# Residual of row blocks 6 and 3 held apart in DRAM and added in SBUF, with plain stores; gates of row block 3 on GpSimd; another order of the last steps

## The chip, the core and the metric

The kernel runs on one NeuronCore of a Trainium2 chip. The core has five instruction streams that run side by side and meet at semaphores: TensorE (PE, with its weight loads shown as PEld), VectorE (DVE), ScalarE (ACT), GpSimd (POOL) and SyncE (SP), which only issues transfers here. Each stream executes its instructions strictly in the order in which the program lists them. Sixteen DMA engines move data between DRAM and the on-chip memory SBUF; matmul results land in PSUM banks of 128x512 float32.

The metric is the device time of one launch in microseconds (us). Before the change it is 1100.19 us, the median of three runs (1099.69 to 1100.69).

## The reference

One layer of a hybrid decoder over 1024 tokens of width 1024, all in float32. Only the last sub-layer matters here:

```python
    h = rmsnorm(x, pre_w_mlp[l]) * (1.0 + sc2) + sh2
    u = jnp.square(jax.nn.relu(h @ w_up[l]))
    x = x + g2 * rmsnorm(u @ w_down[l], post_w_mlp[l])
```

Here `x` on the right is the residual that the first sub-layer produced, and `rmsnorm(y, w)` is `y / sqrt(mean(y^2) + eps) * w`, with the mean over the 1024 columns of a row.

## The kernel before

The 1024 rows (tokens) are cut into eight row blocks, 0 to 7, of 128 rows each; a row block has two halves of 512 columns. The product with `w_down` is computed with a seven-product scheme (Strassen's), which pairs row block t with row block t+4, for t = 0 to 3. `ORDER` names the seven products 1, 5, 6, 3, 7, 2, 4. `PLAN` (L1480) says for each product which PSUM bank it accumulates in ("a", "b" or "c"), whether it starts that bank, and to which accumulator its content is added afterwards. A bank holds a running sum: in bank "a" product 1 is followed by 6, then by 7, then by 4, and after each of these the bank is read out and added to a different accumulator. So product 6 of a pair may not start on PE before DVE has read the bank as product 1 left it. The accumulators are `accs[tb][half]`, 128x512 tiles in SBUF, one for each row block and half.

The contraction runs in five groups of 128-row blocks. The change touches the last group (g = 4, two blocks; each product is six matmuls of 512 columns) and what follows it. The list `order` (L1586) interleaves the products of the pairs t = 0, 1, 2 over steps 0 to 20, and steps 21 to 23 are products 1, 5, 6 of the pair t = 3. `last_rows` (L1621) holds the remaining four products of t = 3 (row blocks 3 and 7) by hand.

At each step the code lists the product's matmuls, then the read-out of the product of the step before (`accum`, DVE: accumulator += bank), then whatever was put down for this step with `on(step, fn)`. When the last addition to a half of a row block is done, a chain of small steps follows, spread over the next steps of the list:

- `square(tb, half)`: ACT squares the half and sums each row (the sum is fetched by a second instruction, ACTIVATION_READ_ACCUMULATOR);
- `gated(tb, half)`: DVE multiplies the half by `gw2`, the product of gate and norm weight, in place, so it must come after the square has read it;
- `root(tb)`: DVE adds the two halves' sums (TENSOR_SCALAR, 128x1), POOL raises the result to the power -0.5;
- `scaled(tb, half)`: ACT multiplies the half by that factor, a scalar for each row;
- `onto_x(tb)`: POOL issues two DMAs that add the halves onto `out` in DRAM, where the residual was stored long before (L1027). POOL is busy while it issues one.

The residual of three halves, (3,1), (7,0) and (7,1), is not stored to `out` but to a DRAM tile `x1d`, and loaded back to SBUF ahead of the end (L1278); there DVE multiplies by the factor and adds the residual in one SCALAR_TENSOR_TENSOR, and SP or ACT issue a plain store.

Engines are pinned, so each runs its instructions in the order of the listing; a scheduler places SP's plain stores. All operations go through one helper (L39), which is therefore the line that the profile shows for nearly everything.

Of the kernel before, what the change touches and what calls it, by code (L numbers as in the profile page):

```python
# [47 lines left out]
def hybrid_layer(ctx: ExitStack, tc: tile.TileContext, I, out, dbg=None):  # L48
# [31 lines left out]
    def m_(name, shape=(P, 512), dt=F32):  # L80
        return M.tile(list(shape), dt, tag="m", name=name)
# [10 lines left out]
    def tp_ps(name):  # L92
        return pb.tile([P, 512], F32, tag="b", name=name)
# [905 lines left out]

    x2ctx = ExitStack()  # L1000
    X2 = x2ctx.enter_context(tc.tile_pool(name="poolX2", bufs=1))
    x1d = dram.tile([P, 3 * 512], F32, tag="x1d", name="x1d")
    hold = {(3, 1): slice(0, 512), (7, 0): slice(512, D), (7, 1): slice(D, D + 512)}
    xn2 = [None] * TB

    def out_proj(tb):
# [264 lines left out]
    for i, (g, n) in enumerate(stages):  # L1271
# [3 lines left out]
        if 10 <= i and gates:  # L1275
            entry_gate(*gates.pop(0))
        ends.append(len(seq))
    for i in range(3):  # L1278
        seq.append((f"x1_{i}", lambda i=i: x1d[:, i * 512:i * 512 + 512], None))

    def load_ahead():
# [339 lines left out]
    def last_rows():  # L1621
        a, b, t = 3, 7, 3
        ss = small.tile([P, 3], F32, tag="ssl", bufs=1, name="ssl")
        one = {n: small.tile([P, 1], F32, tag="l_" + n, bufs=1, name="l_" + n) for n in ("part", "r")}
        h = [slice(0, 512), slice(512, D)]
        ba, bc, bb, bx = bk["a", 3], bk["c", 3], tp_ps("pdlb"), tp_ps("pdlx")
        gl = [m_(f"gl{half}") for half in range(2)]
        ga0, ga = m_("ga0"), m_("ga")
# [20 lines left out]
        rest(nstep + 2)  # L1649
        acp = [accs[b][0][:, 256 * i:256 * i + 256] for i in range(2)]  # L1650
        dmm(bx[:, 0:256], g, 4, t, True, slice(0, 256))
        dmm(bx[:, 256:512], g, 4, t, True, slice(256, 512))
        for step in sorted(later):
            rest(step)
        add(accs[b][1], ba)
        sq(accs[b][1], ss[:, 0:1])
        root(a)
        add(accs[b][0], ba)
        for i in range(2):
            add(acp[i], bx[:, 256 * i:256 * i + 256])  # L1660
            sq(acp[i], ss[:, 1 + i:2 + i], 256)
        ACT.activation(ga0, ga0, AF.Copy, scale=rr_[a][:, 0:1])
        DVE.tensor_tensor(gl[1], accs[b][1], gw2[:, h[1]], ALU.mult)
# [3 lines left out]
        POOL.dma_start(out[a * P:(a + 1) * P, h[0]], ga0, accum_op=ALU.add)  # L1667
        DVE.tensor_tensor(gl[0], accs[b][0], gw2[:, h[0]], ALU.mult)
        xa, xl = take(), [take() for _ in range(2)]
        DVE.scalar_tensor_tensor(ga, ga, rr_[a][:, 0:1], xa, ALU.mult, ALU.add)  # L1670
        nc.sync.dma_start(out[a * P:(a + 1) * P, h[1]], ga)
        for half in range(2):
            DVE.scalar_tensor_tensor(gl[half], gl[half], one["r"][:, 0:1], xl[half], ALU.mult, ALU.add)
            (nc.sync if half else nc.scalar).dma_start(out[b * P:(b + 1) * P, h[half]], gl[half])

    last_rows()

# [66 lines left out]
```

## Time and profile before

| What | Value |
|---|---|
| Time, median of 3 runs | 1100.19 us |
| Span of the profiled execution, first to last instruction | 1097.6 us |
| PE busy | 1076.2 us (98%) |
| DVE busy | 795.1 us (72%) |
| ACT busy | 584.6 us (53%) |
| POOL busy | 373.2 us (34%) |

The profiled execution has its own time, of which the span is what the profile can show. 1097.6 us is 2.6 us below the median of the runs. Differences are worked out in the span and put onto the median. In a timeline row stand the start in us from the span's beginning, the duration in us (for several instructions merged, from the first start to the last end, or their sum), the engine, the line, the operation, out<-in, shapes, the count, and in brackets the idle time before it with what ended it. In a row of windows stand the stretch, its length, the busy time of PE, PEld, DVE, ACT and POOL with the number of instructions in brackets, the granted TensorE clock as a share of full speed, the busy share of the DMA engines and GB/s moved. A DMA issue row gives its queue's engine, the count, the size, and the us from issue to landing.

### The profile page before, as it was taken

The page shows a single profiled execution, that of the slowest core. Times are in us where ns is not written, and L with a number is a line of the kernel's source. Part 1 is how long each engine was busy: PE and PEld are TensorE (multiplying, and loading weights), DVE is VectorE, ACT ScalarE, POOL GpSimd, SP SyncE. Part 2 cuts the span into 40 slices and gives each one's busy share as a digit, 9 for nine tenths or more (in the row PEclk, how much of TensorE's full clock was granted, in tenths as well). Part 3 has the DMA queues.
Part 4 walks back from the last instruction along what each step waited for, and adds up shares of the span by engine and source line. Part 5 has one row for each costly group of instructions (what it writes and reads, how often), then busy time and mean ns, then how long its engine had stood idle before and what let it go on. Part 6 is the DMA issues. An engine that isn't in the chain of part 4 may idle for free.

```text
span 1097.6 us, 16208 instructions
## 1 busy us (share of the span) xinstructions
PE 1076.2 (98%) x5547; PEld 878.2 (80%) x5547; DVE 795.1 (72%) x1323; ACT 584.6 (53%) x1206; POOL 373.2 (34%) x499
## 2 busy tenths in 40 slices
PE   8999999999999999999999999999999999999995
PEld 6788776778888888888888888888888888888884
DVE  4365777878865574559776767876767787899876
ACT  3445544364565764566655555556664543555434
POOL 1153211033324663432543444533333333310014
PEclk9999999999999999999999999999999999999998
DMA  9701301534310352324577676767998888998537
GB/s 347 265 7 57 117 1 43 181 101 140 125 56 11 108 182 96 125 79 144 194 246 249 233 259 227 257 216 244 320 364 289 275 299 259 337 308 272 169 76 131
DMA packets 101587, 203.37 MB, mean 185 GB/s; under 512 B 13025, under 2 KB 13681, under 8 KB 101505
## 3 DMA queue, kind: packets, MB, share of 16 engines
q1 hardware_dynamic: 85968, 154.52, 41.4%
q0 software_dynamic: 15392, 47.57, 14.3%
q8 instruction: 43, 0.70, 0.3%
q14 instruction: 40, 0.32, 0.1%
q10 hardware_dynamic: 144, 0.26, 0.1%
HBM read 147.25 MB, written 55.05 MB: 184 GB/s over the span
## 4 chain that ended last, share of the span: by engine, by line
PE 92%; DVE 3%; ACT 1%; DMA 1%; POOL 1%; issue 1%; SPq 0%; DVEq 0%; POOLq 0%; ACTq 0%
PE pda L39 16%; PE pua L39 14%; PE pdc L39 8%; PE po L39 8%; PE puc L39 7%; PE pu L39 4%; PE pdb L39 4%; PE pq L39 4%; PE phg L39 4%; PE phq L39 3%; PE pub L39 3%; PE phf L39 3%; PE pv L39 3%; PE pk L39 2%; PE o L39 1%; PE sc L39 1%
## 5 line engine op out<-in xcount | busy, mean ns | idle before, releaser
L39 POOL TENSOR_TENSOR b<-b,b 128x512 f32<-128x512 f32 x64 | 89.6, 1400 | 222.8 <-DMA b<-w_dn 222.4
L39 ACT ACTIVATE dw<-dwr 128x512 fp32r<-128x512 f32 x72 | 45.4, 630 | 46.5 <-DMA dwr<-td 32.4
L39 ACT ACTIVATE s<-s 128x512 f32<-128x512 f32 x84 | 53.0, 631 | 31.8 <-DVE s L39 30.5
L39 DVE TENSOR_TENSOR dw<-dwr,dw 128x512 fp32r<-128x512 f32 x72 | 53.6, 744 | 9.0 <-ACT dw L39 8.9
L39 DVE TENSOR_TENSOR acc<-pda,acc 128x512 f32<-128x512 f32 x68 | 46.5, 684 | 13.7 <-PE pda L39 13.3
L39 POOL DMA_DIRECT2D td<-b x64 | 36.3, 567 | 21.6 <-POOL b L39 18.7
L39 POOL TENSOR_TENSOR rrf<-ssf,mhalf 128x1 f32<-128x1 f32 x7 | 7.9, 1253 | 95.3 <-DVE ssf L39 95.3
L39 DVE TENSOR_TENSOR wt<-s,wt 128x512 fp32r<-128x512 f32 x42 | 37.2, 886 | 2.6 <-ACT wt L39 2.5
L39 ACT ACTIVATE s<-pua 128x512 f32<-128x512 f32 x28 | 16.7, 598 | 39.4 <-PE pua L39 33.9
L39 ACT ACT_TABLE_LOAD x28 | 35.9, 1283 | 1.2 <-PEq L1737 0.7
L39 DVE SCALAR_TENSOR_TENSOR macc<-wada,cs,macc 128x512 f32<-128x512 f32 x42 | 33.7, 803 | 3.4 <-DMA wada<-wada 2.9
L39 POOL DMA_DIRECT2D b<-w_dn x64 | 34.4, 540 | 0.0
L39 POOL TENSOR_TENSOR comb<-comb,rd 128x512 f32<-128x512 f32 x8 | 11.7, 1458 | 63.3 <-DVE rd L39 44.2
L39 PE MATMUL pua<-bt_0h,wt 128*128 128x512 f32 x84 | 32.7, 389 | 0.0
L39 PE MATMUL pua<-bt_1h,wt 128*128 128x512 f32 x84 | 32.7, 389 | 0.0
L39 PE MATMUL pua<-bt_3h,wt 128*128 128x512 f32 x84 | 32.7, 389 | 0.0
L39 PE MATMUL pua<-bt_2h,wt 128*128 128x512 f32 x84 | 32.7, 389 | 0.0
L39 DVE TENSOR_TENSOR wt<-a,wt 128x512 fp32r<-128x512 f32 x42 | 31.0, 738 | 0.9 <-ACT wt L39 0.9
L39 DVE TENSOR_TENSOR acc<-pdc,acc 128x512 f32<-128x512 f32 x36 | 24.6, 684 | 8.5 <-PE pdc L39 8.4
L39 ACT ACTIVATE wt<-s 128x512 fp32r<-128x512 f32 x42 | 26.3, 626 | 8.2 <-DVE s L39 8.0
L39 PE MATMUL pda<-dw,du_6h 128*128 128x512 f32 x96 | 29.6, 389 | 0.0
L39 PE MATMUL pda<-dw,du_7h 128*128 128x512 f32 x96 | 29.5, 389 | 0.0
(757 smaller groups left out, 3746.1 us busy)
## 6 DMA issues: line engine op xcount, KB each, us to landing
dur<-ud SPq DMA_DIRECT2D x112, 256.0 KB, 4.5
wada<-wada SPq DMA_DIRECT2D x64, 256.0 KB, 3.5
b<-w_dn POOLq DMA_DIRECT2D x64, 256.0 KB, 5.2
td<-b POOLq DMA_DIRECT2D x64, 256.0 KB, 3.3
dwr<-td SPq DMA_DIRECT2D x64, 256.0 KB, 4.3
a<-w_u SPq DMA_DIRECT2D x56, 256.0 KB, 4.4
dwr<-w_dn SPq DMA_DIRECT2D x48, 256.0 KB, 4.5
ud<-s SPq DMA_DIRECT2D x42, 256.0 KB, 3.6
```

Source lines behind the costliest of these rows:

```text
L39: ins = op(*args, **kw)
```

## The change

Row block 6 (both halves) and half (3,0) join the three halves whose residual is kept in `x1d`: six halves instead of three. They are loaded back by SP, and `with_x` adds them in SBUF, followed by a plain store. So the accumulating DMAs of (6,0), (6,1) and (3,0) are gone, and with them three of ACT's scalings; one scaling, of (3,1), is new, since its residual is added by POOL. The gates of row block 3 move from DVE to POOL. In `last_rows` product 7 comes ahead of 3, product 4 accumulates onto bank "a" in place of a bank of its own (`pdlx`), and row 7's gates come earlier. For pairs t = 0 and 1 `root`, the second gate, `scaled` and `onto_x` move one step earlier; for t = 2 they move by one to two steps and the gates stand directly behind the squares.

```diff
-    x1d = dram.tile([P, 3 * 512], F32, tag="x1d", name="x1d")
-    hold = {(3, 1): slice(0, 512), (7, 0): slice(512, D), (7, 1): slice(D, D + 512)}
+    x1d = dram.tile([P, 6 * 512], F32, tag="x1d", name="x1d")
+    hold = {(tb, half): slice(1024 * i + 512 * half, 1024 * i + 512 * half + 512)
+            for i, tb in enumerate((6, 3, 7)) for half in range(2)}
...
-    for i in range(3):
+    for i in range(6):
         seq.append((f"x1_{i}", lambda i=i: x1d[:, i * 512:i * 512 + 512], None))
...
+    def with_x(tb, half):
+        acc = accs[tb][half]
+        DVE.scalar_tensor_tensor(acc, acc, rr_[tb][:, 0:1], xt[tb, half], ALU.mult, ALU.add)
+        store(tb, half, nc.sync)
...
+        if step == 12:
+            xt = {(tb, half): take() for tb in (6, 3, 7) for half in range(2)}
         if k >= 3 and t < 3:
             tb = t + 4 * th
             on(step + 1, lambda tb=tb, half=half: square(tb, half))
-            if k < 5:
+            if t == 2:
+                on(step + (4 if k == 4 else 2 if k == 3 else 1), lambda tb=tb, half=half: gated(tb, half))
+                if k == 5:
+                    on(step + 1, lambda tb=tb: root(tb))
+                elif k == 6:
+                    on(step + 2, lambda tb=tb: root(tb))
+                    for i, hf in enumerate((half, 1 - half)):
+                        on(step + 3 + i, lambda tb=tb, hf=hf: with_x(tb, hf))
+            elif k < 5:
                 on(step + 3, lambda tb=tb, half=half: gated(tb, half))
             else:
-                on(step + 3, lambda tb=tb: root(tb))
-                on(step + 3, lambda tb=tb, half=half: gated(tb, half))
+                on(step + 2, lambda tb=tb: root(tb))
+                on(step + 2, lambda tb=tb, half=half: gated(tb, half))
+            if k >= 5 and tb != 6:
                 for hf in (1 - half, half):
-                    on(step + 4, lambda tb=tb, hf=hf: scaled(tb, hf))
-                on(step + 5, lambda tb=tb: onto_x(tb))
+                    on(step + (2 if t == 2 else 3), lambda tb=tb, hf=hf: scaled(tb, hf))
+                on(step + (3 if t == 2 else 4), lambda tb=tb: onto_x(tb))
...
-        dmm(bc, g, 3, t, False)
+        dmm(ba, g, 7, t, False)
         add(accs[a][0], bb)
         square(a, 0)
+        POOL.tensor_tensor(accs[a][0], accs[a][0], gw2[:, 0:512], ALU.mult)
         rest(nstep + 1)
-        dmm(ba, g, 7, t, False)
-        add(accs[a][1], bc)
-        square(a, 1)
-        DVE.tensor_tensor(ga0, accs[a][0], gw2[:, h[0]], ALU.mult)
-        DVE.tensor_tensor(ga, accs[a][1], gw2[:, h[1]], ALU.mult)
+        dmm(bc, g, 3, t, False)
+        add(accs[b][1], ba)
+        sq(accs[b][1], ss[:, 0:1])
+        gated(b, 1)
         rest(nstep + 2)
-        dmm(bx[:, 0:256], g, 4, t, True, slice(0, 256))
-        dmm(bx[:, 256:512], g, 4, t, True, slice(256, 512))
+        halves = [slice(0, 256), slice(256, 512)]
+        for c in halves:
+            dmm(ba[:, c], g, 4, t, False, c)
...
+        add(accs[a][1], bc)
+        square(a, 1)
+        POOL.tensor_tensor(accs[a][1], accs[a][1], gw2[:, 512:D], ALU.mult)
+        for i, c in enumerate(halves):
+            add(accs[b][0][:, c], ba[:, c])
+            sq(accs[b][0][:, c], ss[:, 1 + i:2 + i], 256)
         root(a)
+        gated(b, 0)
...
+        scaled(a, 1)
+        with_x(a, 0)
+        POOL.tensor_tensor(accs[a][1], accs[a][1], xt[a, 1], ALU.add)
+        store(a, 1, nc.sync)
         for half in range(2):
-            DVE.scalar_tensor_tensor(gl[half], gl[half], one["r"][:, 0:1], xl[half], ALU.mult, ALU.add)
-            (nc.sync if half else nc.scalar).dma_start(out[b * P:(b + 1) * P, h[half]], gl[half])
+            acc = accs[b][half]
+            DVE.scalar_tensor_tensor(acc, acc, rr_[b][:, 0:1], xt[b, half], ALU.mult, ALU.add)
+            store(b, half, nc.sync if half else nc.scalar)
```

What this does to the streams is seen in the order of instructions. In these rows `acc6_0` is the accumulator of row block 6, half 0 (the last number is only a serial number); `pda4_2` is bank "a" of pair t = 2, `pdc4_3` bank "c" of pair 3, `pdlb` the bank of product 2 of pair 3; `gw2` is the gate, `fin` the square's scratch, `ssf22` and `ssf2` sums of squares of row block 2, `rrf2` its factor, `x1_0` a loaded residual. In square brackets stand the engines or DMA queues whose semaphores the instruction waits for.

First place: DVE from step 19 of `order` on, before the change.

```order
L39 TENSOR_TENSOR acc5_0_8679<-acc5_0_8679,gw2_5244 128x512 [waits DVE_49]
L39 TENSOR_TENSOR acc2_0_8060<-pdb4_2_10831,acc2_0_8060 128x512 [waits PE_49]
L39 TENSOR_TENSOR acc2_1_8277<-acc2_1_8277,gw2_5244 128x512 [waits Activation_49]
L39 TENSOR_TENSOR acc6_0_8705<-pda4_2_10737,acc6_0_8705 128x512 [waits PE_49]
L39 TENSOR_TENSOR acc6_1_8173<-acc6_1_8173,gw2_5244 128x512 [waits Activation_49]
L39 TENSOR_TENSOR acc3_0_8092<-pda4_3_10861,acc3_0_8092 128x512 [waits PE_49]
L39 TENSOR_SCALAR ssf2_10882<-ssf22_10828 128x1 [waits Activation_49,Pool_49]
L39 TENSOR_TENSOR acc2_0_8060<-acc2_0_8060,gw2_5244 128x512 [waits DVE_49]
L39 TENSOR_TENSOR acc7_1_8199<-pdc4_3_10874,acc7_1_8199 128x512 [waits PE_49]
L39 TENSOR_SCALAR ssf6_10896<-ssf26_10846 128x1 [waits Activation_49,Pool_49]
L39 TENSOR_TENSOR acc6_0_8705<-acc6_0_8705,gw2_5244 128x512 [waits DVE_49]
```

And DVE at the same place with the change.

```order
L39 TENSOR_TENSOR acc2_1_8277<-acc2_1_8277,gw2_5244 128x512 [waits Activation_49]
L39 TENSOR_TENSOR acc2_0_8060<-pdb4_2_10844,acc2_0_8060 128x512 [waits PE_49]
L39 TENSOR_TENSOR acc2_0_8060<-acc2_0_8060,gw2_5244 128x512 [waits Activation_49]
L39 TENSOR_SCALAR ssf2_10870<-ssf22_10841 128x1 [waits Pool_49]
L39 TENSOR_TENSOR acc6_0_8705<-pda4_2_10745,acc6_0_8705 128x512 [waits PE_49]
L39 TENSOR_TENSOR acc6_0_8705<-acc6_0_8705,gw2_5244 128x512 [waits Activation_49]
L39 TENSOR_TENSOR acc3_0_8092<-pda4_3_10874,acc3_0_8092 128x512 [waits PE_49]
L39 TENSOR_TENSOR acc6_1_8173<-acc6_1_8173,gw2_5244 128x512
L39 TENSOR_SCALAR ssf6_10898<-ssf26_10855 128x1 [waits Pool_49]
L39 TENSOR_TENSOR acc7_1_8199<-pdc4_3_10887,acc7_1_8199 128x512 [waits PE_49]
L39 SCALAR_TENSOR_TENSOR acc6_0_8705<-acc6_0_8705,rrf6_10899,x1_0_10601 128x512 [waits DMAHW0_49,Pool_49]
L39 TENSOR_TENSOR acc3_1_8319<-pda4_3_10874,acc3_1_8319 128x512 [waits PE_49]
```

The gates of (2,0) and (6,0) moved up to stand directly behind the read-out of the same half, and wait for ACT there; the read-out of `pda4_3` into `acc3_0` stands behind both. The gate of (6,1) moved behind it. The factor times (6,0) plus the residual comes ahead of the read-out into `acc3_1`.

Second place: ACT in the same stretch, before the change.

```order
L39 ACTIVATE acc5_1_8146<-acc5_1_8146,rrf5_10842 128x512 [waits Pool_49]
L39 ACTIVATE acc5_0_8679<-acc5_0_8679,rrf5_10842 128x512 [waits DVE_49]
L39 ACTIVATE fin2_0_10859,ssf22_10828<-acc2_0_8060 128x512 [waits DVE_49,Activation_49]
L39 ACTIVATE fin6_0_10872,ssf26_10846<-acc6_0_8705 128x512 [waits DVE_49,Activation_49]
L39 ACTIVATE acc2_1_8277<-acc2_1_8277,rrf2_10883 128x512 [waits Pool_49]
L39 ACTIVATE acc2_0_8060<-acc2_0_8060,rrf2_10883 128x512 [waits DVE_49]
L39 ACTIVATE acc6_1_8173<-acc6_1_8173,rrf6_10897 128x512 [waits Pool_49]
L39 ACTIVATE acc6_0_8705<-acc6_0_8705,rrf6_10897 128x512 [waits DVE_49]
```

And ACT with the change.

```order
L39 ACTIVATE acc5_1_8146<-acc5_1_8146,rrf5_10837 128x512 [waits Pool_49]
L39 ACTIVATE acc5_0_8679<-acc5_0_8679,rrf5_10837 128x512 [waits DVE_49]
L39 ACTIVATE fin6_1_10856,ssf26_10855<-acc6_1_8173 128x512 [waits DVE_49,Activation_49]
L39 ACTIVATE fin2_0_10867,ssf22_10841<-acc2_0_8060 128x512 [waits DVE_49,Activation_49]
L39 ACTIVATE acc2_1_8277<-acc2_1_8277,rrf2_10871 128x512 [waits Pool_49]
L39 ACTIVATE acc2_0_8060<-acc2_0_8060,rrf2_10871 128x512 [waits DVE_49]
L39 ACTIVATE fin6_0_10884,ssf26_10855<-acc6_0_8705 128x512 [waits DVE_49,Activation_49]
L39 ACTIVATE fin3_0_10932,ssf23_10931<-acc3_0_8092 128x512 [waits DVE_49,Activation_49]
```

The two scalings of row block 2 moved ahead of the square of (6,0), and the two of row block 6 are gone.

Third place: POOL's last instructions, before the change.

```order
L39 TENSOR_TENSOR rrf2_10883<-ssf2_10882,mhalf_105 128x1 [waits DVE_49]
L39 TENSOR_TENSOR rrf6_10897<-ssf6_10896,mhalf_105 128x1 [waits DVE_49]
L39 DMA out<-acc2_0_8060 128x512 [waits DMASW2_49,Activation_49]
L39 DMA out<-acc2_1_8277 128x512 [waits DMASW3_49]
L39 DMA out<-acc6_0_8705 128x512 [waits DMASW4_49,Activation_49]
L39 DMA out<-acc6_1_8173 128x512 [waits DMASW5_49]
L39 TENSOR_TENSOR rrf3_10960<-ssf3_10959,mhalf_105 128x1 [waits DVE_49]
L39 TENSOR_TENSOR l_r_10903<-l_part_10902,mhalf_105 128x1 [waits DVE_49]
L39 DMA out<-ga0_10908 128x512 [waits DMASW6_49,Activation_49]
```

And POOL with the change.

```order
L39 TENSOR_TENSOR rrf2_10871<-ssf2_10870,mhalf_105 128x1 [waits DVE_49]
L39 DMA out<-acc2_0_8060 128x512 [waits DMASW2_49,Activation_49]
L39 DMA out<-acc2_1_8277 128x512 [waits DMASW3_49]
L39 TENSOR_TENSOR rrf6_10899<-ssf6_10898,mhalf_105 128x1 [waits DVE_49]
L39 TENSOR_TENSOR acc3_0_8092<-acc3_0_8092,gw2_5244 128x512 [waits Activation_49]
L39 TENSOR_TENSOR acc3_1_8319<-acc3_1_8319,gw2_5244 128x512 [waits Activation_49]
L39 TENSOR_TENSOR rrf3_10968<-ssf3_10967,mhalf_105 128x1 [waits DVE_49,Pool_49]
L39 TENSOR_TENSOR l_r_10913<-l_part_10912,mhalf_105 128x1 [waits DVE_49]
L39 TENSOR_TENSOR acc3_1_8319<-acc3_1_8319,x1_3_10657 128x512 [waits DMAHW3_49,Activation_49]
```

Three accumulating DMAs are gone, and two gates and one addition of 128x512 are new; POOL's last DMA now is that of (2,1). SP's last five instructions are now the plain stores of (6,0), (6,1), (3,1), (3,0) and (7,1), in this order, and three more loads of residuals stand ahead of them; ACT still issues the store of (7,0).

More of the change, by code (lines that the diff above doesn't have):

```diff
@@ L1624, in last_rows @@
         one = {n: small.tile([P, 1], F32, tag="l_" + n, bufs=1, name="l_" + n) for n in ("part", "r")}
[L1625 to L1628, printed above, removed]
+        ba, bc, bb = bk["a", 3], bk["c", 3], tp_ps("pdlb")
         def sq(acc, col, w=512):
@@ L1639, in last_rows @@
         rest(nstep)
-        dmm(bc, g, 3, t, False)
+        dmm(ba, g, 7, t, False)
         add(accs[a][0], bb)
         square(a, 0)
+        POOL.tensor_tensor(accs[a][0], accs[a][0], gw2[:, 0:512], ALU.mult)
         rest(nstep + 1)
-        dmm(ba, g, 7, t, False)
+        dmm(bc, g, 3, t, False)
+        add(accs[b][1], ba)
+        sq(accs[b][1], ss[:, 0:1])
+        gated(b, 1)
+        rest(nstep + 2)
+        halves = [slice(0, 256), slice(256, 512)]
+        for c in halves:
+            dmm(ba[:, c], g, 4, t, False, c)
+        for step in sorted(later):
+            rest(step)
         add(accs[a][1], bc)
         square(a, 1)
-        DVE.tensor_tensor(ga0, accs[a][0], gw2[:, h[0]], ALU.mult)
-        DVE.tensor_tensor(ga, accs[a][1], gw2[:, h[1]], ALU.mult)
-        rest(nstep + 2)
-        acp = [accs[b][0][:, 256 * i:256 * i + 256] for i in range(2)]
-        dmm(bx[:, 0:256], g, 4, t, True, slice(0, 256))
-        dmm(bx[:, 256:512], g, 4, t, True, slice(256, 512))
[L1653 to L1656, printed above, removed]
-        root(a)
[L1658 to L1663, printed above, removed]
+        POOL.tensor_tensor(accs[a][1], accs[a][1], gw2[:, 512:D], ALU.mult)
+        for i, c in enumerate(halves):
+            add(accs[b][0][:, c], ba[:, c])
+            sq(accs[b][0][:, c], ss[:, 1 + i:2 + i], 256)
+        root(a)
+        gated(b, 0)
         DVE.tensor_scalar(one["part"], ss[:, 0:1], ss[:, 1:2], D * EPS, ALU.add, ALU.add)
@@ L1666, in last_rows @@
         POOL.tensor_tensor(one["r"], one["part"], mhalf[:, 0:1], ALU.pow)
[L1667 to L1671, printed above, removed]
+        rr_[b] = one["r"]
+        scaled(a, 1)
+        with_x(a, 0)
+        POOL.tensor_tensor(accs[a][1], accs[a][1], xt[a, 1], ALU.add)
+        store(a, 1, nc.sync)
         for half in range(2):
-            DVE.scalar_tensor_tensor(gl[half], gl[half], one["r"][:, 0:1], xl[half], ALU.mult, ALU.add)
-            (nc.sync if half else nc.scalar).dma_start(out[b * P:(b + 1) * P, h[half]], gl[half])
+            acc = accs[b][half]
+            DVE.scalar_tensor_tensor(acc, acc, rr_[b][:, 0:1], xt[b, half], ALU.mult, ALU.add)
+            store(b, half, nc.sync if half else nc.scalar)
     last_rows()
```

## The prediction, made before the changed kernel had run

> **What bounds the kernel now.** I read the page first, then the last 20 us in windows, timelines, DMA issues and the rows of the closing line L1740.
>
> ```profile
> span 1097.6 us, 16208 instructions
> PE 1076.2 (98%) x5547; PEld 878.2 (80%) x5547; DVE 795.1 (72%) x1323; ACT 584.6 (53%) x1206; POOL 373.2 (34%) x499
> PE 92%; DVE 3%; ACT 1%; DMA 1%; POOL 1%; issue 1%; SPq 0%; DVEq 0%; POOLq 0%; ACTq 0%
> ...
> 1084.40 0.28 PE L39 MATMUL pdlx<-dw,du_4l 128*128 128x256 f32 x1
> 1089.62 0.34 SPq L1674 DMA_DIRECT2D out<-gl  x1
> out<-gl SPq DMA_DIRECT2D x1, 256.0 KB, 4.7
> L1740 SPq DRAIN  x3: 7/7/7, 1094.5 to 1097.1; - x3
> 1087.97 0.88 POOL L39 DMA_DIRECT2D out<-ga  x1
> out<-ga POOLq DMA_DIRECT2D x1, 256.0 KB, 5.7
> L1740 POOLq DRAIN  x3: 46/99/9116, 1087.7 to 1097.3; - x3
> L1740 DVEq DRAIN  x2: 19/802/1584, 1088.1 to 1097.1; - x2
> ```
>
> PE is the bound up to its last matmul, which ends at 1084.68; any stall of PE is paid in full. Behind it lie 12.9 us in three pieces. From 1084.68 to the last store's issue at 1089.62 the chain runs through DVE, ACT and POOL: 4.9 us. That store lands 4.7 us later, at 1094.3, and SP is through with its waits 0.3 us after (its DRAIN at 1094.5). But the span does not end there: POOL's DRAIN starts at 1087.7, takes 9.116 us and ends at 1096.8, 8.0 us behind the end of POOL's last accumulating DMA issue (1087.97 + 0.88) and 3.1 behind its landing (1087.97 + 5.7 = 1093.7). Only 0.8 us follow. So 2.2 us (1096.8 less 1094.6) are owed to POOL alone.
>
> ```profile
> 1076.00:1080.00 4.00, 4.00 (x19) 3.30 (x19) 3.46 (x8) 2.26 (x6) 2.77 (x4) 1.00 0.94 140
> 1092.00:1093.00 1.00, 0.00 (x0) 0.00 (x0) 0.00 (x0) 0.00 (x0) 0.00 (x0) 0.50 1.09 336
> 1093.00:1094.00 1.00, 0.00 (x0) 0.00 (x0) 0.00 (x0) 0.00 (x0) 0.00 (x0) 0.50 0.52 195
> ud<-rl SPq DMA_DIRECT2D x6, 256.0 KB, 2.0
> ```
>
> The DMA engines are full (share about 1) from 1076 to 1093, at 140 GB/s while only accumulating DMAs run and up to 336 when plain stores are left. A plain 256 KB store that meets no queue lands in 2.0 us, so the last one loses 2.7 us in the queue.
>
> **What the change takes off.** Three accumulating DMAs go. Row 2's pair becomes the last, and the final four stores meet an empty queue. I worked the chain through (below): they are issued at 1095.5, 1095.9, 1096.1 and 1096.7. A store alone needs 2.0 us; the four move 1.05 MB, 3.1 us at 336 GB/s. Thus the last lands between 1098.7 and 1099.8; I take 1099.6, near the queued end, that is 2.9 us behind the last issue in place of 4.7: **-1.8 us**. POOL's last DMA is issued some 13 us before POOL's last addition; I take it that its DRAIN then ends with that addition, as DVE's DRAIN of 1.584 us ends with DVE's work, so the end is landing + 0.3 + 0.8: **-2.2 us** (bounds: all of it, or nothing, rival 2).
>
> **What the change adds on PE.** Here is the hand-over between ACT, DVE and POOL as it is now.
>
> ```profile
> 1075.59 1.34 ACT L39 ACTIVATE acc<-acc,rrf 128x512 f32<-128x512 f32 x2 [1.32 <-POOL rrf L39]
> 1076.83 0.58 ACT L39 ACTIVATE fin<-acc 128x512 f32<-128x512 f32 x1
> 1077.35 0.19 ACT L39 ACTIVATION_READ_ACCUMULATOR fin<-acc 128x1 f32 x1
> 1077.57 0.60 ACT L39 ACTIVATE fin<-acc 128x512 f32<-128x512 f32 x1
> 1080.21 2.57 ACT L39 ACTIVATE acc<-acc,rrf 128x512 f32<-128x512 f32 x4 [1.92 <-POOL rrf L39]
> ...
> 1073.77 0.69 DVE L39 TENSOR_TENSOR acc<-pdb,acc 128x512 f32<-128x512 f32 x1
> 1075.13 0.69 DVE L39 TENSOR_TENSOR acc<-pda,acc 128x512 f32<-128x512 f32 x1
> 1075.74 0.68 DVE L39 TENSOR_TENSOR acc<-acc,gw 128x512 f32<-128x512 f32 x1
> 1076.49 0.69 DVE L39 TENSOR_TENSOR acc<-pda,acc 128x512 f32<-128x512 f32 x1
> 1077.65 0.21 DVE L39 TENSOR_SCALAR ssf<-ssf 128x1 f32<-128x1 f32 x1 [0.47 <-ACT fin L39]
> ...
> 1070.30 0.20 DVE L39 TENSOR_SCALAR ssf<-ssf 128x1 f32<-128x1 f32 x1
> 1070.59 0.94 POOL L39 TENSOR_TENSOR rrf<-ssf,mhalf 128x1 f32<-128x1 f32 x1 [1.00 <-DVE ssf L39]
> L39 POOL TENSOR_TENSOR rrf<-ssf,mhalf 128x1 f32<-128x1 f32 x7 | 7.9, 1253 | 95.3 <-DVE ssf L39 95.3
> ...
> 1077.42 0.39 PE L39 MATMUL pdc<-dw,du_5l 128*128 128x512 f32 x1
> 1077.65 0.62 PE L39 MATMUL pda<-dw,du_6h 128*128 128x512 f32 x2
> ```
>
> Today DVE reads product 1 of pair 3 out of its bank at 1076.49 to 1077.18, and PE puts product 6 onto that bank at 1077.65: 0.47 us to spare. The wait for ACT comes after the read-out. With the change two gates that wait for ACT stand ahead of it. Step by step, each step of `order` taking 1.36 us on PE:
>
> - Row 5's scalings start one step earlier, 1075.59 - 1.36 = 1074.23, and take 1.26. Then ACT squares (6,1) at 1075.49 and (2,0) at 1076.25 (0.76 each, as from 1076.83 to 1077.57). The sum of (2,0) is fetched by 1076.98.
> - DVE has read out (2,0) at 1073.77 or a little later, and its gate waits until 1077.0. At 0.60 a start, the sum's addition follows at 1077.6 and the read-out of (6,0) at 1077.75, in place of 1075.13.
> - POOL's power starts 0.09 after the addition (0.21) and takes 0.94: 1078.86. ACT scales row 2 from 1078.9 to 1080.16, and only then squares (6,0); its sum is fetched by 1080.88.
> - DVE's gate of (6,0) starts at 1080.9, the read-out of product 1 at 1081.5, and ends at 1082.2. PE's product 6 starts at 1082.3 in place of 1077.65.
>
> That is a stall of about 4.5 us, with a further 0.1 at step 20, where product 4 of pair 2 waits for (6,1)'s read-out, which now stands behind row 5's gate. A third follows at product 7 of pair 3: DVE reads product 6 out only behind (6,0) + residual, which waits for row 6's power (1083.0 + 0.94); the read-out ends at 1085.4, and PE would be free at 1085.0: 0.5. Together PE's last matmul ends at 1089.8: **+5.1 us**. Bounds: 0.94 is the short end of the power's durations, and its group's mean of 1.25 at the two powers in these waits gives +5.7; downward the end is no stall at all (rival 3). I take 5.1, since every duration in it is from a row of the very same instruction, and POOL has nothing else to do at either place.
>
> **The tail behind PE.** It has new work on POOL.
>
> ```profile
> L39 POOL TENSOR_TENSOR b<-b,b 128x512 f32<-128x512 f32 x64 | 89.6, 1400 | 222.8 <-DMA b<-w_dn 222.4
> 955.10 1.30 POOL L39 TENSOR_TENSOR b<-b,b 128x512 f32<-128x512 f32 x1
> 955.29 1.67 DVE L39 TENSOR_TENSOR du_2l<-dur,du_2h 128x512 fp32r<-128x512 f32 x1
> 1087.53 0.74 DVE L39 SCALAR_TENSOR_TENSOR ga<-ga,rrf,x 128x512 f32<-128x512 f32 x1
> ```
>
> A POOL operation of this shape takes 1.3 alone; and a DVE operation with two SBUF inputs that starts 0.19 behind one takes 1.67 in place of 0.68, ending 0.56 after POOL's. Behind PE's end at 1089.8: DVE's last additions to row 7 end at 1090.6, ACT's three squares at 1092.0; POOL gates (3,1) until 1092.2, takes two powers until 1094.1 and adds (3,1)'s residual until 1095.4. SP stores (3,1), (3,0) and (7,1) in this order. DVE's last two operations fall under POOL's addition and end at 1096.0 and 1096.7. So the last issue is 6.9 us behind PE in place of 4.9: **+2.0 us** (+1.4 if they do not collide). Saved on the way: one DVE addition (0.60) and two ACT scalings, which nobody waits for.
>
> At no cost: three loads more on SP,
>
> ```profile
> 1049.00:1056.00 7.00, 7.00 (x33) 5.79 (x32) 5.26 (x9) 1.77 (x4) 0.00 (x0) 1.00 0.00 0
> x<-x1d SPq DMA_DIRECT2D x3, 256.0 KB, 3.6
> ```
>
> which run in a stretch where DMA is idle and land some 20 us before they are read; uncovered they would be 3.6. The stores to `x1d` replace stores of the same size.
>
> **Sum.** +5.1 + 2.0 - 1.8 - 2.2 = +3.1 us on the span of 1097.6: 1100.7. The median of the runs is 2.6 above the span, so 1100.19 + 3.1 = **1103.3 us**.
>
> **The rivals.** (1) The clock falls in the stall.
>
> ```profile
> 1084.70:1088.62 3.92, 0.00 (x0) 0.00 (x0) 3.69 (x9) 2.17 (x7) 2.84 (x4) 1.00 1.06 151
> 1088.62:1097.60 8.98, 0.00 (x0) 0.00 (x0) 0.97 (x2) 0.00 (x0) 0.24 (x1) 0.50 0.59 145
> ```
>
> The granted clock went from 1.00 to 0.50 just 3.9 us after the last matmul. PE would stand idle from 1077.9 to 1082.3, 4.4 us. If the clock falls there, matmuls take about twice as long for some 3 to 6 us: +1.4 to +3.0, say 1105.4. One fall seen once at 3.9 speaks for it, the narrow margin against it. The Trainium skill, TensorE: Matmul & The Clock Gate, section What's actually happening, says that the fall comes after a whole idle window of 3.4 us whose windows run free of the program. By that rule (4.4 - 3.4)/3.4, an estimate of 0.3, is the chance for each execution, and a median would mostly not show it; by the row alone it would happen each time. The row's 3.9 lies within what the page allows. I give it 0.25.
>
> (2) POOL's DRAIN keeps its 8.0 us behind POOL's last work whatever that is: 1095.4 + 8.0 + 0.8 = 1104.2, or 1106.8 on the median. For it: only one long DRAIN is seen; against it: POOL's two other DRAINs are of 0.1 us. 0.08.
>
> (3) Faster: the ACT-DVE loop closes in time. Its place is the gate of (6,0); if ACT gets to that square before 1076, the read-out is not late, PE's 5.1 goes, and the rest gives +2.0 - 1.8 - 2.2 or a little more: 1097.5. It decides at a PE stall of 0 to 1 us, where the sum passes -2.2. Against it stand the order rows of both engines. 0.12, of which 0.08 beyond 0.2%.
>
> That the change does not do what it says is excluded by the rows of POOL and SP.
>
> **How the numbers follow.** The forecast has 0.55, for 1101.5 to 1105; 0.12 of it lies within 0.2% (2.2 us, about what a measurement can tell from no change). So faster 0.08, same 0.16, slower 0.76. The range 1098.5 to 1106.5 leaves out most of rival 3 and rival 2.
>
> **What would show it.** PE idle some 4.4 us ahead of pda<-du_6, released by DVE; DVE idle 2 to 3 us ahead of two gates, released by ACT fin; ACT idle near 1.9 us ahead of row 2's scalings; the last four stores landing in 2 to 4 us; POOL's long DRAIN short. A PE without that gap makes the prediction wrong, and so does a span that ends 8 us behind POOL.

## The result, and the profile after

The changed kernel takes 1106.32 us (median of 5 runs, 1105.92 to 1108.71) beside 1099.69 us for the kernel before (5 runs, 1098.93 to 1100.69): a ratio of 1.0062, 95% interval 1.005 to 1.0074, **6.6 us slower** where 3.1 were forecast. The direction and the stall were right; two terms of the sum were wrong. The profiled execution is the longest of the five, 1108.71 us, and 2.15 us of it are lost ahead of the last rows (PE starts the product on `pdb<-dw,du_2h` of pair 2 at 1074.36 in place of 1072.21), which belong to this execution and not to the change: in e4 below, whose kernel is the same up to that place, the product starts at 1072.07. The comparisons below leave them out.

The page of the changed kernel, its span, busy times, chain, and the rows of the closing line, now L1754:

```profile
span 1106.8 us, 16213 instructions
...
PE 1079.3 (98%) x5547; PEld 879.1 (79%) x5547; DVE 794.4 (72%) x1322; ACT 583.2 (53%) x1204; POOL 376.0 (34%) x499
...
PE 87%; DVE 4%; DMA 3%; ACT 2%; issue 1%; POOL 1%; SPq 0%; DVEq 0%; ACTq 0%; POOLq 0%
```

```profile
L1754 POOLq DRAIN  x3: 46/99/7821, 1098.2 to 1106.6; - x3
L1754 SPq DRAIN  x3: 7/7/7, 1103.7 to 1106.3; - x3
```

The span holds 9.2 us more than before, and the shares hardly show it: PE's share of the chain fell from 92% to 87%, and its busy time is 3 us *larger* with the same number of matmuls. Matmuls that take longer are the first hint at the clock. The timelines of PE, DVE and ACT around the wait (start, duration, instruction, and in brackets the idle time ahead of it and its releaser):

```profile
1079.87 0.39 PE L39 MATMUL pdc<-dw,du_5l 128*128 128x512 f32 x1
1084.41 1.22 PE L39 MATMUL pda<-dw,du_6h 128*128 128x512 f32 x2 [4.15 <-DVE acc L39]
1085.42 0.63 PE L39 MATMUL pda<-dw,du_6l 128*128 128x512 f32 x1
...
1087.13 1.05 PE L39 MATMUL pdlb<-dw,du_2h 128*128 128x512 f32 x2
...
1089.69 0.84 PE L39 MATMUL pda<-dw,du_7h 128*128 128x512 f32 x2
...
1076.34 0.69 DVE L39 TENSOR_TENSOR acc<-pdb,acc 128x512 f32<-128x512 f32 x1
1079.58 0.69 DVE L39 TENSOR_TENSOR acc<-acc,gw 128x512 f32<-128x512 f32 x1 [2.56 <-ACT fin L39]
1080.19 0.21 DVE L39 TENSOR_SCALAR ssf<-ssf 128x1 f32<-128x1 f32 x1
1080.32 0.68 DVE L39 TENSOR_TENSOR acc<-pda,acc 128x512 f32<-128x512 f32 x1
1083.06 0.69 DVE L39 TENSOR_TENSOR acc<-acc,gw 128x512 f32<-128x512 f32 x1 [2.06 <-ACT fin L39]
1083.67 0.68 DVE L39 TENSOR_TENSOR acc<-pda,acc 128x512 f32<-128x512 f32 x1
...
1078.83 0.60 ACT L39 ACTIVATE fin<-acc 128x512 f32<-128x512 f32 x1
...
1081.08 1.33 ACT L39 ACTIVATE acc<-acc,rrf 128x512 f32<-128x512 f32 x2 [1.53 <-POOL rrf L39]
1082.32 0.58 ACT L39 ACTIVATE fin<-acc 128x512 f32<-128x512 f32 x1
```

Read it from below: ACT waits for POOL's power before it scales row 2, squares (6,0) only then, at 1082.32; DVE's gate of (6,0) waits for that square until 1083.06, and the read-out of product 1 behind the gate, which is what PE needs, comes at 1083.67. PE's product 6 starts at 1084.41. The step ahead of it (1078.73, a product of 1.36) was through at 1080.09, so 4.32 us are lost. Then look at the durations: product 2 on `pdlb` takes 2.56 us (1087.13 to 1089.69) for the same six matmuls that take 1.36 elsewhere. The windows of this stretch give the reason (length, busy time of PE, PEld, DVE, ACT, POOL with instructions, granted PE clock, DMA share, GB/s):

```profile
1080.26:1084.41 4.15, 0.00 (x1) 0.01 (x1) 2.09 (x6) 1.94 (x4) 2.26 (x4) 0.87 0.89 124
1084.41:1090.15 5.74, 5.74 (x14) 4.48 (x15) 3.59 (x7) 0.00 (x0) 0.65 (x2) 0.50 0.80 171
1090.15:1094.25 4.10, 4.10 (x24) 3.44 (x22) 2.37 (x4) 1.45 (x4) 1.28 (x1) 1.00 0.03 10
1094.25:1101.30 7.05, 0.00 (x1) 0.00 (x0) 5.15 (x10) 2.46 (x7) 4.50 (x4) 0.69 0.16 62
1101.30:1106.80 5.50, 0.00 (x0) 0.00 (x0) 0.00 (x0) 0.00 (x0) 0.00 (x0) 0.50 0.29 112
```

The 0.87 of the first row is a mean: the clock is at 1.00 until 1083.33, and at 0.50 from there to 1090.15, 6.83 us. PE works for 5.74 us of them: half of it, 2.87 us, is lost. Behind PE's end at 1094.25 stand these rows of POOL and DVE, and of the last stores' landing:

```profile
1097.44 0.55 POOL L39 TENSOR_TENSOR l_r<-l_part,mhalf 128x1 f32<-128x1 f32 x1
1098.28 1.74 POOL L39 TENSOR_TENSOR acc<-acc,x 128x512 f32<-128x512 f32 x1 [0.29 <-ACT acc L39]
...
1098.15 2.41 DVE L39 SCALAR_TENSOR_TENSOR acc<-acc,l_r,x 128x512 f32<-128x512 f32 x2
...
1100.47 0.89 SPq L1554 DMA_DIRECT2D out<-acc  x2
```

```profile
out<-acc SPq DMA_DIRECT2D x2, 256.0 KB, 2.4
```

The last store is issued at 1100.94, 6.7 us behind PE (4.9 before), and lands 2.4 us later (4.7 before), so SP is through at 1103.7. But the span runs on to 1106.8: POOL's DRAIN starts at 1098.2, takes 7.821 and ends at 1106.06, **6.04 us behind the end of POOL's addition** (1098.28 + 1.74 = 1100.02; the view gives a DRAIN's start to a tenth only, so this and the like figures below are good to 0.05 us). What the store gains, nobody collects. From PE's end to the span's end it is 12.55 us in place of 12.92.

### The profile page after: what moved, and what is told of

Same layout as the page of the kernel before. It is cut to its first block, busy times and chain, and to the rows that moved or that the text cites. A ratio compares the mean times of both kernels' runs of the same rounds, so it can differ in the third digit from the quotient of the medians.

```text
span 1106.8 us, 16213 instructions
## 1 busy us (share of the span) xinstructions
PE 1079.3 (98%) x5547; PEld 879.1 (79%) x5547; DVE 794.4 (72%) x1322; ACT 583.2 (53%) x1204; POOL 376.0 (34%) x499
## 4 chain that ended last, share of the span: by engine, by line
PE 87%; DVE 4%; DMA 3%; ACT 2%; issue 1%; POOL 1%; SPq 0%; DVEq 0%; ACTq 0%; POOLq 0%
PE pua L39 14%; PE pda L39 13%; PE po L39 8%; PE puc L39 7%; PE pdc L39 6%; PE pu L39 4%; PE pq L39 4%; PE pdb L39 4%; PE phg L39 3%; PE phq L39 3%; PE pub L39 3%; PE phf L39 3%; PE pv L39 3%; PE pk L39 2%; PE o L39 1%
## 5 line engine op out<-in xcount | busy, mean ns | idle before, releaser
L39 DVE TENSOR_TENSOR acc<-pda,acc 128x512 f32<-128x512 f32 (+1 forms) x69 | 46.7, 678 | 17.5 <-PE pda L39 17.3
L39 DVE TENSOR_TENSOR s<-puc,s 128x512 f32<-128x512 f32 x14 | 9.7, 691 | 28.7 <-issue 26.2
L39 PE MATMUL pdc<-dw,du_3h 128*128 128x512 f32 x96 | 29.7, 390 | 0.4 <-DVE acc L39 0.4
```

The lines of the kernel that those rows point to most:

```text
L39: ins = op(*args, **kw)
```

## The experiments

Medians are compared with runs of the kernel before on the same chip. Runs e1 to e5 and e7 start from the changed kernel; e6, b0 and b1 start from the kernel before.

**e1: the order of row pair 2 undone, all else kept.**

```diff
-                on(step + (4 if k == 4 else 2 if k == 3 else 1), lambda tb=tb, half=half: gated(tb, half))
-                if k == 5:
-                    on(step + 1, lambda tb=tb: root(tb))
-                elif k == 6:
-                    on(step + 2, lambda tb=tb: root(tb))
-                    for i, hf in enumerate((half, 1 - half)):
-                        on(step + 3 + i, lambda tb=tb, hf=hf: with_x(tb, hf))
+                if k >= 5:
+                    on(step + 3, lambda tb=tb: root(tb))
+                on(step + 3, lambda tb=tb, half=half: gated(tb, half))
+                if k == 6:
+                    for hf in (half, 1 - half):
+                        on(step + 5, lambda tb=tb, hf=hf: with_x(tb, hf))
...
-                    on(step + (2 if t == 2 else 3), lambda tb=tb, hf=hf: scaled(tb, hf))
-                on(step + (3 if t == 2 else 4), lambda tb=tb: onto_x(tb))
+                    on(step + (4 if t == 2 else 3), lambda tb=tb, hf=hf: scaled(tb, hf))
+                on(step + (5 if t == 2 else 4), lambda tb=tb: onto_x(tb))
```

> The changed kernel with the chain of row pair 2 (gates, roots, scalings of row 2, residual of row 6) put back to the steps of the kernel before; plain stores, residual tiles, row 3's work on GpSimd and the order of the last products stay as changed. My theory: the 4.15 us in which PE waits ahead of pda<-du_6 come from DVE's two gates of row pair 2, which wait for ACT ahead of the read-out, and the granted clock of 0.50 from 1083.33 to 1090.15 follows from that idle time. Then both go: no gap of PE over 0.5 us behind 1060, clock 1.00 to the last matmul, which ends near 1084.7 to 1085.2 plus the offset ahead of the tail; time = before + 0.2 (PE) + 1.8 (tail) - 2.3 (landing) = about 1099.4 (1098.5 to 1100.5). Rival A, the stall has another cause (the plain stores or the residual loads hold up the DVE or PE): the gap stays and the time is near 1106. Rival B, POOL's DRAIN ends a fixed 6 us behind POOL's last operation: then it ends 6.0 us behind the last 128x512 addition of POOL. By my theory on it (it ends 2.2 to 2.4 us behind the last landing or SP's own DRAIN) it follows SP.

Measured: 1100.22 us, ratio 1.0002 (0.9994 to 1.0011). PE of e1 around the same product, its windows, and its closing rows:

```profile
1077.89 0.39 PE L39 MATMUL pdc<-dw,du_5l 128*128 128x512 f32 x1
1078.12 0.62 PE L39 MATMUL pda<-dw,du_6h 128*128 128x512 f32 x2
```

```profile
1060.00:1085.40 25.40, 25.40 (x116) 20.46 (x114) 20.04 (x36) 14.21 (x32) 15.39 (x17) 1.00 0.72 106
```

```profile
1089.76 1.74 POOL L39 TENSOR_TENSOR acc<-acc,x 128x512 f32<-128x512 f32 x1 [0.31 <-ACT acc L39]
```

```profile
L1753 POOLq DRAIN  x3: 46/99/7821, 1089.7 to 1098.1; - x3
L1753 SPq DRAIN  x3: 7/7/7, 1095.2 to 1097.8; - x3
```

PE runs through without a gap at full clock, so stall and clock both go with the order: 6.1 us of the 6.6. Rival A falls. All the rest of the change together is worth nothing that the interval can tell from zero. The time is 0.8 above the middle of the expectation, which counted the landing's 2.3 as a gain: POOL's DRAIN, and not SP, sets the end. POOL's DRAIN again ends 6.04 us behind its addition (1091.50; 1089.72 + 7.82 = 1097.54), 2.4 behind SP; so far both theories on it fit.

**e6: that order alone, put into the kernel before.** Gates and roots stand at the steps of the changed kernel, scalings and accumulating DMAs of rows 2 and 6 right behind; no plain store.

```diff
-            if k < 5:
+            if t == 2:
+                on(step + (4 if k == 4 else 2 if k == 3 else 1), lambda tb=tb, half=half: gated(tb, half))
+                if k >= 5:
+                    on(step + (1 if k == 5 else 2), lambda tb=tb: root(tb))
+                    for hf in (1 - half, half):
+                        on(step + (2 if k == 5 else 3), lambda tb=tb, hf=hf: scaled(tb, hf))
+                    on(step + (3 if k == 5 else 4), lambda tb=tb: onto_x(tb))
+            elif k < 5:
```

> The kernel before with one part of the change alone: gates of row pair 2 directly behind their squares, roots of rows 2 and 6 and scalings of rows 2 and 6 two steps or one step earlier; all rows stored as before (accumulating DMAs), last products in the old order. Theory: this part holds the whole loss. PE waits 4 to 4.3 us ahead of pda<-du_6, the clock falls to 0.50 for two windows (6.83 us), 2.3 to 2.9 us of it paid: 1100.2 + 6.5 = 1106.5 (1105.5 to 1107.5). Rival: it needs the plain stores or the residual additions to lose time: 1100 to 1102.

Measured: 1105.47 us, ratio 1.0043 (1.0028 to 1.0058): 5.0 us above the kernel before, just under the range. The wait ahead of `pda<-du_6` was 4.57 us, but the clock fell for half as long, 3.41 us. PE at its restart and the windows of e6:

```profile
1082.33 1.22 PE L39 MATMUL pda<-dw,du_6h 128*128 128x512 f32 x2 [4.57 <-DVE acc L39]
```

```profile
1077.76:1081.94 4.18, 0.00 (x0) 0.00 (x0) 2.14 (x5) 1.95 (x4) 3.52 (x5) 1.00 0.50 70
1081.94:1085.36 3.42, 3.03 (x7) 2.46 (x8) 1.72 (x5) 1.33 (x2) 1.17 (x3) 0.50 1.09 167
```

PE works for 3.0 us of the slow stretch: 1.5 lost in place of 2.9. The order needs no plain store to lose its time.

**e2: PE kept busy in the wait.**

```diff
         flush()
+        if step == 23:
+            pid = tp_ps("pdidle")
+            for _ in range(3):
+                dmm(pid, g, 5, t, True)
         if first:
```

> The changed kernel with 18 more matmuls (three further copies of pair 3's product 5 into a spare bank that nobody reads, 3 x 1.36 = 4.1 us) ahead of pda<-du_6, where PE waits anyway. Theory 'idle PE lowers the granted clock': the clock stays 1.00 to the last matmul, the products behind the wait take 1.36 us each in place of 2.6, and the time is 2.9 us below the changed kernel's: about 1103.4 (1102.5 to 1104). Rival 'the matmuls behind the wait are slow for another cause' (operands, traffic of DMA, DVE and POOL): they stay at 2.6 and the time near 1106.3. Rival 'the copies themselves delay the product': the first matmul of pda<-du_6 starts later than 0.1 us behind DVE's read-out, and the time is 1106 or more.

Measured: 1104.06 us, ratio 1.0045 (1.0031 to 1.0058), 2.3 below the changed kernel where 2.9 were expected, and 0.06 above the range; one of its six executions took 1108.32 us with a mean clock of 0.993. PE of e2 at the end of the copies, and its windows:

```profile
1081.77 0.39 PE L39 MATMUL pdidle<-dw,du_5l 128*128 128x512 f32 x1
1082.24 0.73 PE L39 MATMUL pda<-dw,du_6h 128*128 128x512 f32 x2
...
1083.73 0.62 PE L39 MATMUL pdlb<-dw,du_2h 128*128 128x512 f32 x2
...
1085.09 0.64 PE L39 MATMUL pda<-dw,du_7h 128*128 128x512 f32 x2
```

```profile
1082.00:1085.40 3.40, 3.31 (x15) 2.53 (x15) 3.32 (x7) 0.00 (x0) 0.89 (x2) 1.00 1.05 140
```

The read-out comes as late as before, but in the profiled execution the clock stays at 1.00 and product 2 takes 1.36 again (1083.73 to 1085.09). Useless work made the kernel faster: the slow products were the clock's.

**e7: one copy in place of three**, so that PE idles 2.8 us.

```diff
-            for _ in range(3):
+            for _ in range(1):
```

> As e2, with one copy of product 5 (6 matmuls, 1.36 us) in place of three ahead of pda<-du_6: PE idles about 2.8 us in one piece, in place of 4.15 without copies and 0.1 with three. Three profiles with an idle time of 4.1 to 4.6 us all show the granted clock at 0.50 behind it, one with 1.4 us shows none; in two of the three the window of 3.41 us ahead of the fall still held 0.2 to 0.3 us of PE's work. Theory 'the fall needs a window of 3.41 us that is nearly all idle': with 2.8 idle a window holds at least 0.6 us of work, the clock stays 1.00 in most executions: about 1104 as e2, mean granted clock 0.996. Rival 'a fall needs only about 2.5 us of idle time': 1105.5 to 1106.5, mean clock 0.992 to 0.995. A mixture from one execution to the next would show that the place of the window decides.

Measured: 1106.97 us, ratio 1.0065 (1.0052 to 1.0079). It looks like the mixture: one execution took 1103.8 us with a mean granted clock of 0.996, the four others 1106.5 to 1108.2 with 0.993 to 0.995. The profile caught the first:

```profile
1082.07 0.73 PE L39 MATMUL pda<-dw,du_6h 128*128 128x512 f32 x2 [2.79 <-DVE acc L39]
```

```profile
1082.00:1085.40 3.40, 3.33 (x15) 2.66 (x16) 3.32 (x8) 0.00 (x0) 0.72 (x2) 1.00 0.96 153
```

That the clock fell in the others is read from their times and mean clocks, not from a trace. Two of the mean clocks (0.993) lie below all those of the kernel before in the same session (0.995 and 0.996); the two of 0.995 do not, so for these only the time speaks.

**e3: one gate back.** Only the gate of (6,0), the root of row 6 and row 6's residual come one or two steps later; the gate of (2,0) still waits ahead of the read-out.

```diff
-                on(step + (4 if k == 4 else 2 if k == 3 else 1), lambda tb=tb, half=half: gated(tb, half))
+                on(step + (4 if k == 4 else 2 if k == 3 else 3 if k == 6 else 1), lambda tb=tb, half=half: gated(tb, half))
...
-                    on(step + 2, lambda tb=tb: root(tb))
-                    for i, hf in enumerate((half, 1 - half)):
-                        on(step + 3 + i, lambda tb=tb, hf=hf: with_x(tb, hf))
+                    on(step + 3, lambda tb=tb: root(tb))
+                    for hf in (half, 1 - half):
+                        on(step + 5, lambda tb=tb, hf=hf: with_x(tb, hf))
```

> The changed kernel with only the gate of (6,0), the root of row 6 and row 6's residual put two or three steps later, so that DVE's read-out of product 1 of pair 3 no longer waits for the square of (6,0), but still for the gate of (2,0). Theory: PE's wait ahead of pda<-du_6 shrinks from 4.15 to about 1.4 us (read-out of product 1 ends near 1.5 us behind PE's need), this is too short for the clock to fall, so it stays 1.00: time = 1099.4 + 1.6 = about 1101 (1100 to 1102). Rival, the clock falls after any wait of PE of a microsecond: +2 to +3 more, 1103.5 to 1104. Rival, the wait isn't DVE's order: it stays over 4 us, 1106.

Measured: 1102.12 us, ratio 1.0023 (1.0014 to 1.0031), 1.9 above e1 where 1.6 were expected.

```profile
1079.76 0.73 PE L39 MATMUL pda<-dw,du_6h 128*128 128x512 f32 x2 [1.40 <-DVE acc L39]
```

```profile
1077.00:1082.00 5.00, 3.60 (x17) 2.65 (x16) 4.04 (x9) 2.61 (x6) 3.11 (x5) 1.00 0.79 112
```

The gap is 1.40 us and the clock stays up in the profiled execution, so this wait costs itself. The waits of 4.32 us in the changed kernel and 4.57 us in e6 cost 2.87 and 1.5 us on top.

**e4: SP's queue made longer.** It adds no work on POOL.

```diff
             store(b, half, nc.sync if half else nc.scalar)
+        for i in range(2):
+            nc.sync.dma_start(x1d[:, 0:512], accs[b][1])
+            nc.sync.dma_start(accs[b][1], x1d[:, 0:512])
```

> The changed kernel with four more DMAs on SP's queue behind the last store (out of a finished tile to x1d and back, twice), each waiting for the one ahead of it; the outputs are stored before them as in the changed kernel. SP gets through some 7 us later, POOL does nothing more. Theory 1: the end of POOL's long DRAIN follows SP's end or the last landing, 2.2 to 2.4 us behind SP's DRAIN (as 1096.82 behind 1094.58 before and 1106.06 behind 1103.73 after): it ends about 7 us later than in the changed kernel, some 13 us behind POOL's last addition, and the span grows by the full 7 us. Theory 2 (the prediction's and rival 2's view): it follows POOL's own work alone, 6 us behind its last operation: it ends where it did, and the span grows by about 4.6 us, to 0.8 behind SP's DRAIN.

Measured: one execution, 1111.85 us. POOL's last operation in e4 and the closing rows:

```profile
1096.04 1.74 POOL L39 TENSOR_TENSOR acc<-acc,x 128x512 f32<-128x512 f32 x1 [0.29 <-ACT acc L39]
```

```profile
L1757 POOLq DRAIN  x3: 46/108/7821, 1096.0 to 1109.6; - x3
L1757 SPq DRAIN  x3: 7/7/7, 1109.1 to 1109.4; - x3
```

My theory 1 falls. The DRAIN takes 7.821 us to the nanosecond as in the changed kernel and in e1, and ends at 1103.82, 6.04 behind the addition, while SP works on until 1109.1. The likeness of 2.2 to 2.4 us behind SP in the other three was chance. In e4 SP sets the end, 0.8 ahead of the span's (1109.9).

**e5: e1 without POOL's late addition.**

```diff
-        scaled(a, 1)
         with_x(a, 0)
-        POOL.tensor_tensor(accs[a][1], accs[a][1], xt[a, 1], ALU.add)
-        store(a, 1, nc.sync)
+        with_x(a, 1)
```

> The kernel of e1 (no stall, 1100.2) with (3,1) + residual done by DVE as the three others, in place of ACT's scaling and POOL's addition; POOL's last operation is then the power of row 7. Theory: POOL's DRAIN ends 6.0 us behind POOL's last computation, whatever SP does, and sets the end of the span in e1 (POOL 1097.55, SP 1095.16). Here it ends 6.0 us behind the power, near 1095.5 (2.0 earlier), and DVE's last operation comes some 0.7 us earlier, as nothing collides with it: 1098.2 (1097.5 to 1098.8). Rival, POOL's DRAIN takes 8 us behind a power as it did behind a DMA issue, or SP's end sets the span: only the tail's 0.7 is gained, 1099.5 or the same as e1.

Measured: 1098.43 us, ratio 0.9984 (0.9976 to 0.9993), as expected to 0.2 us.

```profile
1089.36 0.55 POOL L39 TENSOR_TENSOR l_r<-l_part,mhalf 128x1 f32<-128x1 f32 x1
...
1090.74 1.41 DVE L39 SCALAR_TENSOR_TENSOR acc<-acc,l_r,x 128x512 f32<-128x512 f32 x2
```

```profile
L1751 POOLq DRAIN  x3: 46/99/6634, 1089.3 to 1096.5; - x3
L1751 SPq DRAIN  x3: 7/7/7, 1094.6 to 1096.2; - x3
```

The DRAIN again ends 6.04 us behind POOL's last computation (1089.91; 1089.32 + 6.63 = 1095.95), now the short power. And DVE's last pair takes 1.41 in place of 2.41, with one operation more on DVE: the collision was real.

**b0 and b1: plain stores without the order.** b0 is the kernel before with (3,0) kept apart, added by DVE and stored by SP; b1 does the same for row 6 too. Their core, in `last_rows` of b0:

```diff
-        ACT.activation(ga0, ga0, AF.Copy, scale=rr_[a][:, 0:1])
-        POOL.dma_start(out[a * P:(a + 1) * P, h[0]], ga0, accum_op=ALU.add)
+        for half, gt in enumerate((ga0, ga)):
+            DVE.scalar_tensor_tensor(gt, gt, rr_[a][:, 0:1], xa[half], ALU.mult, ALU.add)
+            nc.sync.dma_start(out[a * P:(a + 1) * P, h[half]], gt)
```

> The kernel before, with the order of all steps and products as it was; only the residual of (3,0) is kept apart, added by DVE (one more operation of 0.66 us in the tail) and stored by SP, in place of ACT's scaling and POOL's last accumulating DMA. Rows 6 and 2 are still accumulated. Theory: POOL's last operation is then the power of row 7 (ends 1088.0 before), its DRAIN ends 6.0 us behind, 1094.1 in place of 1096.8; the last issue is 0.7 later, the last landing stays near 1094.3 or is up to 0.7 later; the end is SP's: span 1095.4 to 1096.1, time 1098.3 (1097.5 to 1099). Rival, POOL's DRAIN keeps 8 us behind its last work of any kind: 1096 and 1096.8, time 1099.4. Rival, the store queue behind row 6's accumulations is what counts and moves with the last issue: no gain, 1100.

> As b0, with the residuals of row 6 too kept apart, added by DVE and stored by SP; order of steps and products as before. Theory: no stall of PE; DVE has two operations of 0.66 us more ahead of its last ones, so the last issue is 0.7 to 1.4 later than in the kernel before (1090.3 to 1091.0); it lands 2.4 to 2.9 us later with the queue empty: 1092.9 to 1093.7; POOL's DRAIN ends 6.0 behind the power of row 7 (1088.0 to 1088.7): 1094.1 to 1094.7, and the span 0.8 later: time 1097.8 (1097 to 1098.7). Rival: DVE's two operations hold up a read-out that PE waits for (0.7 or more), or delay the tail by more than the queue gives back: 1099 or slower.

Measured: b0 1097.69 us, ratio 0.9971 (0.9963 to 0.998); b1 1097.89 us, ratio 0.9974 (0.9964 to 0.9984). Both beat the kernel before, by 2.7 and 2.5 us, and the changed one by over 8. POOL's last operation in b0, its closing rows, then the landing of the last store in b0 and in b1:

```profile
1087.52 0.93 POOL L39 TENSOR_TENSOR l_r<-l_part,mhalf 128x1 f32<-128x1 f32 x1 [1.09 <-DVE l_part L39]
```

```profile
L1739 POOLq DRAIN  x3: 46/108/7360, 1087.5 to 1095.4; - x3
L1739 SPq DRAIN  x3: 7/7/7, 1094.4 to 1095.1; - x3
```

```profile
out<-gl SPq DMA_DIRECT2D x1, 256.0 KB, 3.6
...
out<-gl SPq DMA_DIRECT2D x1, 256.0 KB, 2.1
```

In b0 POOL's DRAIN ends at 1094.85, SP is through at 1094.4: the two ends meet. In b1 the last store lands 1.5 us sooner, but it is issued 6.6 us behind PE's end in place of 5.6 (DVE has two operations more), and POOL's DRAIN ends 9.7 us behind PE's end in both; so b1 gains nothing over b0.

## Why the prediction was off

It was right step by step where it followed rows of the order:

- Step 20: 0.1 forecast; 0.15 measured (1075.87 in place of 1074.36 + 1.36), and the product that starts there takes 1.50 in place of 1.36 (its first pair of matmuls is longer), 0.3 in all.
- The stall at `pda<-du_6`: 4.5 forecast; 4.32 measured, released by DVE, with DVE's 2.56 and 2.06 us of waiting for ACT ahead of the two gates and ACT's 1.53 for POOL. That the size fits so well is partly luck. ACT scales row 5 at 1076.85, 0.47 later than forecast (1074.23 + 2.15), as POOL's power for row 5 ends only at 1076.81; and POOL's power for row 2 takes 0.56 in place of the 0.94 that the prediction held for the short end. The two nearly cancel.
- The third stall, 0.5 at product 7, is not there: in e2, with the clock up, product 7 follows at 1083.73 + 1.36 = 1085.09. Row 6's power takes 0.56 there too, and DVE's read-out of product 6 is through at 1084.95.
- The tail: +2.0 forecast, +1.75 measured, collision included. The landing: -1.8 forecast, -2.3 measured.

**The first wrong step is the clock.** The forecast took it as staying up, and gave the fall 0.25, because it weighed a rule against a row and trusted the rule. The Trainium skill, TensorE: Matmul & The Clock Gate, section What's actually happening, names an idle window of 3.4 us that runs free of the program; read as "wholly idle" it gave 0.3. The slow stretch was 3.41 us in e6 and twice that, 6.83, in the changed kernel and in e4: windows of 3.41 agree with the Trainium skill's. But in the changed kernel and in e4 the 3.41 us ahead of the fall still held 0.34 and 0.24 us of PE's work by the profile, which models the ends of matmuls (PE stopped at 1080.26 and 1077.97, the clock fell at 1083.33 and 1081.14), and the fall came all the same; with 2.8 us idle (e7) four executions of five look like it by their times, with 1.4 (e3) the profile shows none. So a window that is mostly idle seems to be enough. Price: 2.87 us in the profiled execution, 2.3 between the medians (e2).

The traces also suggest why e6 paid only half of that. Of the first slow window of 3.41 us PE was at work for 3.02 us in e6 (from 1081.94), and the clock came back at its end. It was at work for 2.33 us in the changed kernel (from 1083.33) and for 2.43 us in e4 (from 1081.14), and a second slow window followed. So waits of much the same length cost 1.5 or 2.9 us on top, it seems by where their end falls in a window; these are three traces, and no run set that place on purpose.

**The second is POOL's DRAIN, -2.2 forecast, nothing earned.** The prediction took POOL's DRAIN to end with POOL's last addition, since POOL's last DMA lay 13 us back. It ends 6.04 us behind POOL's last computation in the changed kernel, e1, e4 and e5, and in b1 too (1090.25 + 0.55 = 1090.80; 1090.2 + 6.63 = 1096.8). In three other traces POOL's last DMA is later or slower, and there the DRAIN ends 3.0 to 3.2 us behind that DMA's landing: before (1087.97 + 5.7 = 1093.7; 1096.8), e6 (1094.19 + 5.0 = 1099.2; 1093.9 + 8.46 = 1102.4) and b0 (1084.1 + 7.7 = 1091.8; 1094.85). The 8.0 behind the end of the DMA's issue, on the other hand, is 7.3 in e6. So the later of these two ends fits every trace looked at here; no run varied the landing alone. The change has that landing early, and then the 6.04 decide.

Rival 2, with 0.08, was right that the DRAIN closes a fixed time behind POOL's last work; its price was 8.0 where 6.04 is right. That its 1106.8 lies near the measured 1106.32 is luck: it has no fall of the clock, and 2 us too much of the DRAIN. In the changed kernel POOL's last work ends 5.8 us behind PE's end (4.2 before), and so the shorter DRAIN and the later work nearly cancel: 12.55 in place of 12.92 us behind PE.

With both terms put right the sum is 0.3 + 4.32 + 2.87 - 0.37 = 7.1 us for the profiled executions, whose spans, less the 2.15, lie 7.05 apart; the medians lie 6.6 apart. The landing's -2.3 is real and unpaid, as SP was not the last.

What stays open: what POOL does in its DRAIN, how much work in a window keeps the clock up, and how much brings it back; the runs give only the points above.

## What to carry to other kernels

An instruction that waits for another engine must not stand in an in-order queue ahead of the read-out that frees a bank for PE: here the loss was gone with the gate behind the read-out (e1). Price a stall of PE as long as those here (2.8 us and more) with the clock's fall; where it couldn't be avoided, useless matmuls in it were cheaper than the idle time (e2). Before a tail is shortened, ask for each engine when its last work ends and what closes behind it: here POOL's DRAIN ended 6 us behind POOL's last computation, and to move the last addition from POOL to DVE gained 1.8 us (e5).

## What was not expected of the hardware

POOL's DRAIN takes the same 7.821 us in four kernels whose last POOL operation is the same addition of 1.74 us (the changed kernel, e1, e3 and e4), whether SP is through 2.3 us before it ends (changed kernel) or 5.3 us after (e4). The clock comes back after one slow window of 3.41 us in which PE worked for 3.02 us (e6), and not after one with 2.33 (changed kernel). Three copies of a product that nobody reads brought the median from 1106.32 to 1104.06 us.
